# A recurrence stage woven by hand on TensorE, with keys normalised by features

## The chip, the core and the metric

The kernel runs on one core of a Trainium2 chip. A core has TensorE (PE), VectorE (DVE), ScalarE (ACT), GpSimd (POOL) and SyncE (SP), which here issues the loads; each engine works through its own instructions in order and waits on semaphores for the others. The metric is the time of one execution in device microseconds, in the median of several runs.

## What is computed

Two blocks follow each other. The first, which the change touches, projects 528 rows of 1024 features and runs a convolution branch and an RWKV-7 recurrence beside each other; the second (two layers of attention and a mixture of experts) is left as it was. All is fp32. The part that matters:

```python
h = layer_norm(concat([meta, x]))                  # 528 x 1024
p = h @ w_in                                       # conv, r k v, decay/rate/gate, gates
y_conv = conformer_conv(p[..., :c_end])            # GLU, 31 taps, layer norm over features, silu
# rwkv7_time_mix, 16 heads of 64:
p = p + (token_shift(p) - p) * mu
kk = k * k_k
kk = kk / maximum(sqrt(sum(kk * kk, axis=-1)), 1e-12)      # per head
k  = k * (1 + (a - 1) * k_a)
S_t = S_{t-1} diag(decay_t) + (S_{t-1} a_t) b_t^T + v_t k_t^T ;  y_t = S_t r_t   # a = -kk, b = kk * a
o = layer_norm(o) + sum(r * k * r_k) * v ;  o = o * g
y = sigmoid(gate1) * y_conv + sigmoid(gate2) * (o @ w_out)
```

## The kernel before

The recurrence is done in chunks of 64 rows (nine per head, the first half empty), for eight pairs of heads. Every pair j goes through these functions, and a loop of ten steps in first_block calls them for different pairs: at step s, rw_b, rw_solve and rw_bonus for pair s-1, then rw_merge, rw_c and rw_out for pair s-2, then rw_a for pair s.

- rw_a (L358) makes three dense products (k, r, v) of 128 features with all 528 rows, each through token_shift (L289) and dense_ft (L279), then the decays (lw, cum), the keys' squares sq and their sums over a head (ss, L404: five products with two columns), the factor rn per row and head (L410, L411) and the two operands BKf (L426) and AR (L427). A dense product in fp32 is 2 halves of 264 columns x 8 k-tiles x 3 matmuls (hi x hi, lo x hi, hi x lo; L154 to L156), 48 in all.
- rw_b (L445) multiplies AR with BKf per chunk (gr, L460), scales and masks every 128x128 result on DVE (G, L463, 18 of them), writes two parts of G to DRAM (dA, L467) and reads them back in another layout (Dt, L474). It transposes v and BKf (vt, bkt, L480 to L490; BK is scaled by rn at L491) and forms px and at.
- rw_solve (L516) inverts the 16x16 triangles: 15 pairs of a product and a sum on DVE (L524, L525), each on the result of the last; its result goes through DRAM (img) too. rw_merge (L540) builds 64x64 inverses out of them (pm).
- rw_c (L584) forms pB, pG, pM, pN and then a chain of seven small products pS (L642), each with an update of S on DVE (L643), then psy. rw_out (L657) normalises (gsm, gvar, yc) and transposes back (yt, L677).
- The same steps carry the convolution: conv_ft (two dense products), conv_taps (L710: 27 operations cacc over 128x516 on DVE for each of eight filters, L724), conv_norm (L740: the mean and then the variance over all features, each by products as, L737), and gate_ft (16 products in the last steps).
- ada (L1200) hands out weight slabs of the second block: one adw buffer of 512 KB, 8 small matmuls (L1163), a copy adm, and after each second slab two transposes (L1172) and sums on DVE. Nine slabs go with a step.

PSUM has two buffers for dense products (mm), two for the recurrence's g tiles, two for c (pS, yt, pb), one for psy's halves each and one for ada. What orders the instructions is the Tile framework's scheduler with costs of its own: for every engine, PE included, it picks what it holds to be ready, so the functions of one step are interleaved by it. SP issues all loads in one order.

Of the kernel before, what the change touches and what calls it, by code (L numbers as in the profile page):

```python
# [43 lines left out]
            {"yh0": 1, "yl0": 1, "S0": 1, "xg0": 1})  # L44
ADA_FRONT, ADA_EACH, ADA_CONV, ADA_MID = 12, 1, 3, 10
# [27 lines left out]
class K:  # L73
# [204 lines left out]

    def dense_ft(self, ws, m0, m, xs, halves, sink, kts=range(KT), tag="mm"):  # L279
# [78 lines left out]
    def rw_a(self, j):  # L358
# [11 lines left out]
        for q, dst in ((1, k[:, PADL:]), (0, r[:, PADL:]), (2, v[:, 64 + PADL:])):  # L370
            ws = self.weights()
            self.token_shift(ws, 0, 128, 8 * q + j, dst)
            self.ada(ADA_EACH)
# [4 lines left out]


# [17 lines left out]
        kk = wt("kk")  # L397
        nc.scalar.activation(kk, k, AF.Copy, scale=self.col("k_k", j))
        sq = wt("sq")
        nc.scalar.activation(sq, kk, AF.Square)  # L400
        ss = self.psm.tile([128, 512], F32, name="ss", tag="g")
# [3 lines left out]
        rn = self.rn[j % 2]  # L405
        s["rn"] = rn
        st = rw.tile([128, 5, 2], F32, name="sst", tag="sst")
        ssv = ss[:, 0:10].rearrange("p (m h) -> p m h", h=2)
        for lo, hi, m in ((0, 64, 5), (64, 128, 4)):
            nc.vector.tensor_scalar(st[lo:hi, 0:m], ssv[lo:hi, 0:m], 1e-24, 2.0, op0=ALU.max, op1=ALU.mult)  # L410
            nc.vector.reciprocal(rn[lo:hi, lo // 64::2, :], st[lo:hi, 0:m])  # L411
# [5 lines left out]
        nc.vector.scalar_tensor_tensor(b, ta, 1.0, kk, op0=ALU.add, op1=ALU.mult)  # L417
# [27 lines left out]
    def rw_b(self, j):  # L445
# [3 lines left out]
        BKf, AR, rn, v = s["BKf"], s["AR"], s["rn"], s["v"]  # L449
# [4 lines left out]
        for c0 in range(0, 9, 4):  # L454
# [20 lines left out]
        s["Dt"] = Dt  # L475
        for g in range(2):
# [28 lines left out]
        for lo, c0 in ((0, 2), (64, 1)):  # L505
            nc.scalar.activation(UV[lo:lo + 64, c0::2], ps[lo:lo + 64], AF.Copy)
# [508 lines left out]
    def first_block(self):  # L1015
# [51 lines left out]
        for step in range(10):  # L1067
            if 1 <= step <= 8:
                self.rw_b(step - 1)
# [1036 lines left out]
```

## Time and profile before

| | us |
|---|---|
| runs (median of 3) | 4317.6 (4300.29 to 4318.19) |
| profiled execution: time, span | 4312.15, 4310.3 |
| granted PE clock, mean over the span | 0.955 |
| PE, DVE, ACT, POOL busy in the span | 3913.5, 1976.4, 1271.9, 489.9 |
| PE and DVE busy, 209.1 to 639.5 us | 362.60, 335.11 of 430.40 |

The stage of the change runs from about 112 to 896 us. "Busy" of PE counts pipelined matmuls whose ends are modelled; the granted clock is the share of 2.4 GHz, so 0.50 is 1.2 GHz. Idle time is put down to the semaphore that came last. The first gr of the eight pairs started at 150.7, 209.1, 298.7, 382.1, 467.7, 549.8, 639.5 and 734.4 us; "a step" below is the time between two of them.

### The profile page before, as it was taken

Reading aid. Unit: us, or ns where it says so; the run is one execution under the profiler, and the core shown is the slowest. Engines: PE = TensorE matmul, PEld = TensorE weight load, DVE = VectorE, ACT = ScalarE, POOL = GpSimd, SP = SyncE. Lnnn points to the kernel's source line nnn. Section 1 sums busy time; section 2 is a strip of 40 time slices with the busy share of each in tenths; the row PEclk is TensorE's granted clock in tenths of the full one; section 3 lists DMA queues with packets and bytes.
Section 4 is the critical chain, followed back from the end, with each engine's and each line's share of the span. In section 5 each row is a group of like instructions: output and inputs, shape, how many; then the busy total and the mean of one; then the engine's idle time right before and its main releaser. Section 6 shows DMA issues by size and latency. Waiting matters only on the chain. (4 is left out here: it accounts for less than half of the span.)

```text
span 4310.3 us, 68272 instructions
## 1 busy us (share of the span) xinstructions
PE 3913.5 (91%) x28323; PEld 2835.7 (66%) x28323; DVE 1976.4 (46%) x4067; ACT 1271.9 (30%) x2361; POOL 489.9 (11%) x472
## 2 busy tenths in 40 slices
PE   6888888888999899999999899999899999879887
PEld 4767777788998678777878544334577777643322
DVE  4777777644554443445436422213433554432222
ACT  3333333433553333333222211111333332221111
POOL 0322222222010010000003100000010000300000
PEclk9989888999999999999999899999999999989999
DMA  7544454555333222121243698788432124589998
GB/s 233 150 133 121 113 138 135 144 169 164 122 94 102 84 70 64 53 63 53 86 156 118 251 361 323 299 332 318 150 78 65 59 77 147 187 322 409 409 409 333
DMA packets 618041, 764.24 MB, mean 177 GB/s; under 512 B 65593, under 2 KB 463919, under 8 KB 617731
## 3 DMA queue, kind: packets, MB, share of 16 engines
q1 hardware_dynamic: 603699, 722.52, 49.7%
q0 software_dynamic: 6720, 24.87, 1.6%
q10 hardware_dynamic: 7312, 12.48, 0.8%
q8 instruction: 223, 3.65, 0.4%
q14 instruction: 87, 0.71, 0.1%
HBM read 700.45 MB, written 59.33 MB: 176 GB/s over the span
## 5 line engine op out<-in xcount | busy, mean ns | idle before, releaser
L120 DVE TENSOR_TENSOR wlo<-raw,whi 128x1024 fp32r<-128x1024 f32 (+2 forms) x283 | 339.5, 1200 | 606.1 <-ACT whi L118 599.0
L154 PE MATMUL mm<-h2T_hi,whi 128*128 128x512 f32 (+1 forms) x1488 | 526.4, 354 | 2.6 <-ACT kT L1353 2.6
L154 PE MATMUL mm<-hT_hi,whi 128*128 128x258 f32 (+1 forms) x1776 | 521.3, 294 | 5.0 <-ACT gt L775 3.7
L156 PE MATMUL mm<-h2T_hi,wlo 128*128 128x512 f32 (+1 forms) x1488 | 524.0, 352 | 0.0
L155 PE MATMUL mm<-h2T_lo,whi 128*128 128x512 f32 (+1 forms) x1488 | 523.3, 352 | 0.0
L156 PE MATMUL mm<-hT_hi,wlo 128*128 128x258 f32 (+1 forms) x1776 | 518.4, 292 | 1.6 <-DVE wlo L120 1.6
L155 PE MATMUL mm<-hT_lo,whi 128*128 128x258 f32 (+1 forms) x1776 | 517.7, 292 | 0.9 <-POOL hT_lo L786 0.9
L118 ACT ACTIVATE whi<-raw 128x1024 fp32r<-128x1024 f32 (+2 forms) x311 | 306.3, 985 | 686.0 <-PE mm L155 578.2
L1732 PE MATMUL h<-we,xin 128*64 128x512 f32 x1960 | 477.6, 602 | 14.7 <-DMA we<-in_w_e_dram 14.7
L154 PEld LDWEIGHTS mm<-hT_hi,whi 128*128 128x128 f32 x1776 | 342.8, 193 | 13.7 <-issue 4.7
L156 PEld LDWEIGHTS mm<-hT_hi,wlo 128*128 128x128 f32 x1776 | 343.3, 193 | 6.5 <-DVE wlo L120 2.0
L155 PEld LDWEIGHTS mm<-hT_lo,whi 128*128 128x128 f32 x1776 | 343.7, 194 | 5.7 <-issue 2.4
L1732 PEld LDWEIGHTS h<-we,xin 128*64 128x64 f32 x1960 | 143.6, 137 | 291.1 <-issue 253.2
L154 PEld LDWEIGHTS mm<-h2T_hi,whi 128*128 128x128 f32 x1488 | 282.3, 190 | 48.3 <-issue 10.1
L1732 PE MATMUL ye<-we,hT 128*64 128x512 f32 (+1 forms) x2048 | 303.5, 494 | 10.1 <-ACT hT L1809 8.1
L155 PEld LDWEIGHTS mm<-h2T_lo,whi 128*128 128x128 f32 x1488 | 282.4, 190 | 38.7 <-issue 7.6
L156 PEld LDWEIGHTS mm<-h2T_hi,wlo 128*128 128x128 f32 x1488 | 282.4, 190 | 38.3 <-issue 6.5
L1732 PEld LDWEIGHTS ye<-we,hT 128*64 128x64 f32 (+1 forms) x2048 | 103.5, 124 | 184.7 <-issue 128.6
L724 DVE SCALAR_TENSOR_TENSOR cacc<-cc,cdw,cacc 128x516 f32<-128x516 f32 x216 | 178.1, 825 | 3.1
L1804 DVE TENSOR_TENSOR s<-h,s 128x512 f32<-128x512 f32 x32 | 22.1, 692 | 341.3 <-PE h L1732 341.3
L1824 ACT ACTIVATE yh<-y 64x512 fp32r<-64x512 f32 (+1 forms) x128 | 66.7, 521 | 350.9 <-DVE y L1817 348.9
L1817 DVE SCALAR_TENSOR_TENSOR y<-ye,gate,gr 128x512 f32<-128x512 f32 (+1 forms) x48 | 31.7, 661 | 219.6 <-PE ye L1732 219.5
(531 smaller groups left out, 6556.1 us busy)
## 6 DMA issues: line engine op xcount, KB each, us to landing
we<-in_w_e_dram SPq DMA_DIRECT2D x363, 1024.0 KB
raw<-in_w_in_dram SPq DMA_DIRECT2D x170, 512.0 KB
adw<-in_w_ada_dram SPq DMA_DIRECT2D x96, 512.0 KB
raw<-in_ffn_up_dram SPq DMA_DIRECT2D x44, 512.0 KB
raw<-in_w_branch_dram SPq DMA_DIRECT2D x48, 256.0 KB
cres<-in_w_e_dram SPq DMA_DIRECT2D x11, 1024.0 KB
we<-in_w_e_dram POOLq DMA_DIRECT2D x10, 1024.0 KB, 21.2
g_d<-g SPq DMA_DIRECT2D x24, 384.0 KB
```

What stands on the lines that cost most here:

```text
L118: nc.scalar.activation(hi, raw, AF.Copy)
L120: eng.tensor_tensor(lo, raw, hi.bitcast(F32), op=ALU.subtract)
L154: mm(ps, wh, xh, start=(i == 0), stop=False)
L155: mm(ps, wh, xl, start=False, stop=False)
L156: mm(ps, wl, xh, start=False, stop=(i == last))
L724: nc.vector.scalar_tensor_tensor(acc, tap(t), col(t), acc, op0=ALU.mult, op1=ALU.add)
L1732: mm(out[p.cap * g:p.cap * g + p.cap, 0:W], lhs(k), rhs(k)[:, W * d:W * d + W], start=k == 0, stop=k == KT - 1, tile_position=(0, p.cap * g))
L1804: nc.vector.tensor_tensor(s1, p.h3[:, 0:W], s1, op=ALU.mult)
L1817: nc.vector.scalar_tensor_tensor(y, ye[:, 0:W], p.gate, p.gr[:, turn], op0=ALU.mult, op1=ALU.mult)
L1824: nc.scalar.activation(p.yh[r, d], y[r], AF.Copy)
```

## The change

PE's order in the stage is now written out. The pieces of rw_b, rw_merge, rw_c and rw_out become generators; weave (new) takes them in turn from a list, and after every piece it draws one or two units of dense work (nine, nine or six matmuls) from a second generator, fillers, which holds the step's dense products. WEAVE gives the units per step. The loop has 11 steps; rw_out runs one step later, its normalisation is moved to the end of rw_c; rw_solve is emitted right behind the Dt loads; conv_norm starts at step 9, in three parts, and the last filter's taps are emitted ahead of step 8. ada's slabs are drawn inside the dense products' sinks.

The keys are normalised by features: the squares are summed by a product with a block matrix bones, so that the sum stands in every feature row, and the reciprocal multiplies kk there. BKf holds it then, and G is only masked (4 chunks in one operation) and BK only copied, on ACT.

```diff
+WEAVE = (30, 30, 30, 30, 30, 30, 30, 42, 36, 48, 0)
...
+    def dense_units(self, ws, m0, m, xs, halves, sink, tag="mm"):
+        for i, (t0, n) in enumerate(halves):
+            ps = self.psm.tile([128, 512], F32, name="mm", tag=tag)
+            for k in range(KT):
...
+                mm(out, wh, xh, start=k == 0, stop=False)
+                mm(out, wh, xl, start=False, stop=False)
+                mm(out, wl, xh, start=False, stop=k == KT - 1)
+                if k in (2, 5):
+                    yield
+            sink(i, ps[0:m, 0:n], t0, n)
+            yield
...
+        rnb = wt("rnb")
+        for t0 in (0, NTT // 2):
+            ss = self.psm.tile([128, 512], F32, name="ss", tag="mm")
+            mm(ss[:, 0:NTT // 2], self.cst["bones"], sq[:, t0:t0 + NTT // 2], start=True, stop=True)
+            nc.vector.tensor_scalar(rnb[:, t0:t0 + NTT // 2], ss[:, 0:NTT // 2], 1e-24, 2.0, op0=ALU.max, op1=ALU.mult)
+        nc.vector.reciprocal(rnb, rnb)
+        nc.vector.tensor_tensor(rnb, rnb, kk, op=ALU.mult)
...
-        for m in range(5):
-            n = 128 if m < 4 else 64
-            mm(ss[0:n, 2 * m:2 * m + 2], sq[:, 128 * m:128 * m + n], self.cst["hsel"], start=True, stop=True)
...
-            nc.vector.tensor_scalar(st[lo:hi, 0:m], ssv[lo:hi, 0:m], 1e-24, 2.0, op0=ALU.max, op1=ALU.mult)
-            nc.vector.reciprocal(rn[lo:hi, lo // 64::2, :], st[lo:hi, 0:m])
...
-        nc.vector.scalar_tensor_tensor(b, ta, 1.0, kk, op0=ALU.add, op1=ALU.mult)
+        nc.vector.scalar_tensor_tensor(b, ta, 1.0, rnb, op0=ALU.add, op1=ALU.mult)
...
-            for i in range(n):
-                for h in range(2):
-                    nc.vector.scalar_tensor_tensor(G[:, c0 + i, h], ps[h][:, i], rn[:, c0 + i, h:h + 1], self.cst["gmask"], op0=ALU.mult, op1=ALU.mult)
+            for h in range(2):
+                nc.vector.tensor_tensor(G[:, c0:c0 + n, h], ps[h][:, 0:n], self.cst["gmask"].unsqueeze(1).to_broadcast([128, n, 128]), op=ALU.mult)
+            yield
...
         s["Dt"] = Dt
+        self.rw_solve(j)
...
-            nc.vector.tensor_tensor(
-                BK[:, c0:c0 + n].rearrange("p c (h f) -> p c h f", h=2), ps[:, 0:n].rearrange("p c (h f) -> p c h f", h=2),
-                rn[:, c0:c0 + n].unsqueeze(3).to_broadcast([128, n, 2, 64]), op=ALU.mult)
+            nc.scalar.activation(BK[:, c0:c0 + n], ps[:, 0:n], AF.Copy)
+            yield
...
+    def fillers(self, step):
+        if step < 8:
+            yield from self.rw_a(step)
+        if step < 10:
+            for f in CONV[step + 1]:
+                yield from self.conv_ft(f)
+            for f in range(GATES[step], GATES[step + 1]):
+                yield from self.gate_ft(f)
+
+    def weave(self, step):
+        early = self.rw_b(step - 1) if 1 <= step <= 8 else iter(())
+        late = self.rw_late(step - 2) if 2 <= step <= 9 else iter(())
+        out = self.rw_out(step - 3) if step >= 3 else iter(())
+        turns = [early, late, early, out, late, early, late, early, late, early, late, early, late, early, early, late, early, late, early]
+        turns += [late] * 9
+        if step == CONV_NORM + 1:
+            norm = self.conv_norm()
+            turns = [norm] + turns[0:8] + [norm] + turns[8:] + [norm]
...
+        for i, g in enumerate(turns):
+            if next(g, done) is done:
+                continue
+            want = units * (i + 1) // len(turns) - units * i // len(turns)
+            for _ in range(want):
+                next(fill, None)
+        for g in [early, late, out, fill]:
+            for _ in g:
+                pass
...
+        with self.tc.manual_schedule(engines={PE}):
+            self.pinned = True
+            for step in range(11):
+                if step == CONV_NORM:
+                    for f in pending:
+                        self.conv_taps(f)
+                    pending = []
+                self.weave(step)
+                for f in pending:
+                    self.conv_taps(f)
+                pending = CONV[step + 1] if step < 10 else []
```

How this moves instructions is seen at two places. The first is VectorE in a middle step, from behind the masks of one pair to the start of its solve. In the kernel before (bons is the bonus of the pair, k a shifted projection, T and Tt the inverses of the pair ahead, Xt the solve):

```order
L1177 TENSOR_TENSOR mod_214<-mod_214,adb_211 128x2
L442 TENSOR_TENSOR bons<-pb,v 128x258 x2
L724 SCALAR_TENSOR_TENSOR cacc<-cc,cdw,cacc 128x516
L301 SCALAR_TENSOR_TENSOR k<-praw,par,ptmp 128x528
L724 SCALAR_TENSOR_TENSOR cacc<-cc,cdw,cacc 128x516 x3
L565 TENSOR_TENSOR T<-pm_5763,T 128x512
L568 TENSOR_TENSOR Tt<-pm_5780,Tt 32x8x32 x2
L724 SCALAR_TENSOR_TENSOR cacc<-cc,cdw,cacc 128x516
L524 TENSOR_TENSOR Xt<-X_1068,Dt 72x1
L724 SCALAR_TENSOR_TENSOR cacc<-cc,cdw,cacc 128x516
L525 TENSOR_REDUCE X_1068<-Xt 72x1
```

Here taps (cacc) stand on both sides of the solve's first operations. In the changed kernel (pm and T again of the pair ahead, mod an ada result):

```order
L498 TENSOR_TENSOR G<-gr,cst_fb 128x128 x2
L122 TENSOR_TENSOR wlo<-raw,whi 128x1024
L412 SCALAR_TENSOR_TENSOR k<-praw,par,ptmp 128x528
L626 COPY T<-pm_4641 32x8x32 x2
L1259 TENSOR_REDUCE mod_213<-ada 128x2
L1259 TENSOR_REDUCE mod_214<-ada 128x2
L1260 TENSOR_TENSOR mod_213<-mod_213,adb_211 128x2
L1260 TENSOR_TENSOR mod_214<-mod_214,adb_211 128x2
L565 TENSOR_TENSOR Xt<-X_1067,Dt 72x1
L566 TENSOR_REDUCE X_1067<-Xt 72x1
L565 TENSOR_TENSOR Xt<-X_1067,Dt 72x2x2
```

The last two masks are followed by other stages' results and then by the solve without a tap between them; the taps have moved behind it.

The second place is PE around a pair's first gr in a middle step. Before:

```order
L155 MATMUL mm<-hT_lo,whi 128x264
L156 MATMUL mm<-hT_hi,wlo 128x264
L1172 MATMUL ada<-cst_both,adm 128x128 x2
L460 MATMUL gr<-AR,BKf 128x128 x8
L1163 MATMUL ada<-adw,cT 32x128 x8
L460 MATMUL gr<-AR,BKf 128x128 x8
L1163 MATMUL ada<-adw,cT 32x128 x8
L1172 MATMUL ada<-cst_both,adm 128x128 x2
L460 MATMUL gr<-AR,BKf 128x128 x2
L480 MATMUL vt<-cst_both,v 128x128 x4
L484 MATMUL vt<-cst_both,v 128x128
```

The three groups of gr stand close together, with ada slabs between and no dense product. In the changed kernel:

```order
L1246 MATMUL ada<-adw,cT 32x128 x8
L1255 MATMUL ada<-cst_both,adm 128x128 x2
L1246 MATMUL ada<-adw,cT 32x128 x8
L496 MATMUL gr<-AR,BKf 128x128 x8
L295 MATMUL mm<-hT_hi,whi 128x264
L296 MATMUL mm<-hT_lo,whi 128x264
L297 MATMUL mm<-hT_hi,wlo 128x264
```

Two ada slabs now stand directly ahead of the first gr with only the transposes between them, and behind it comes a piece of nine dense matmuls (mm, of which the first three rows are shown) before anything else of the pair.

## Rows read from the trace of the kernel before

**Rows 1.** Windows of the stage: columns as in the line on top (us).
```profile
core 0: us, PE busy (x) PEld busy (x) DVE busy (x) ACT busy (x) POOL busy (x), PEclk, DMA share, GB/s
209.10:639.50 430.40, 362.60 (x4656) 311.64 (x4656) 335.11 (x765) 150.02 (x304) 116.56 (x135) 0.89 0.47 126
...
150.70:209.10 58.40, 51.47 (x513) 44.94 (x512) 53.41 (x121) 21.03 (x41) 21.92 (x22) 0.97 0.55 149
...
639.50:734.40 94.90, 81.86 (x1005) 69.83 (x1005) 72.87 (x163) 30.75 (x65) 21.94 (x23) 0.85 0.46 126
734.40:895.60 161.20, 136.36 (x1669) 124.49 (x1669) 100.61 (x208) 66.57 (x126) 33.49 (x26) 0.94 0.52 150
```

**Rows 2.** Windows inside one step, same columns.
```profile
293.00:300.00 7.00, 1.33 (x12) 1.36 (x12) 6.88 (x11) 0.42 (x1) 4.93 (x8) 0.50 0.13 31
...
316.00:324.00 8.00, 8.00 (x83) 6.22 (x84) 4.92 (x11) 2.07 (x6) 0.00 (x0) 0.52 0.36 82
324.00:330.00 6.00, 6.00 (x118) 4.76 (x115) 4.47 (x8) 2.87 (x7) 0.19 (x1) 1.00 0.42 119
```

**Rows 3.** Groups on VectorE, 112 to 875 us; busy, mean ns, idle before and releaser.
```profile
L724 DVE SCALAR_TENSOR_TENSOR cacc<-cc,cdw,cacc 128x516 f32<-128x516 f32 x216 | 178.1, 825 | 3.1
L524 DVE TENSOR_TENSOR Xt<-X,Dt 72x1 f32<-72x1 f32 (+14 forms) x120 | 50.7, 422 | 1.8
L120 DVE TENSOR_TENSOR wlo<-raw,whi 128x1024 fp32r<-128x1024 f32 x34 | 42.8, 1258 | 11.2 <-ACT whi L118 9.1 <-PE mm L156 1.9
L463 DVE SCALAR_TENSOR_TENSOR G<-gr,rn,cst_fb 128x128 f32<-128x128 f32 x144 | 40.3, 341 | 7.8 <-PE gr L460 7.8
...
L643 DVE SCALAR_TENSOR_TENSOR S<-pS,pcs,S 128x64 f32<-128x64 f32 x56 | 15.7, 281 | 15.7 <-PE pS L642 15.3
L491 DVE TENSOR_TENSOR BK<-bkt,rn 128x512 f32<-128x512 f32 (+1 forms) x24 | 13.1, 554 | 12.4 <-PE bkt L490 12.4
...
L415 DVE TENSOR_TENSOR m<-k,m 128x576 f32<-128x576 f32 x8 | 6.1, 757 | 0.2
...
L565 DVE TENSOR_TENSOR T<-pm,T 128x512 f32<-128x512 f32 x8 | 5.5, 689 | 1.3 <-PE pm L560 1.2
...
L411 DVE RECIPROCAL rn<-sst 64x10 f32<-64x10 f32 (+1 forms) x16 | 3.3, 203 | 0.5
```

**Rows 4.** Groups on VectorE over the whole span: another reciprocal.
```profile
L1502 DVE RECIPROCAL sm<-sm 128x2 f32<-128x2 f32 x40 | 6.6, 165 | 45.3 <-ACT P L1500 45.3
```

**Rows 5.** Waits of PE, 112 to 895 us: total, times, longest (us).
```profile
PE yt L677 <- DVE yc L673: 23.1, 8, 5.4
PE ada L1163 <- DMA adw<-in_w_ada_dram: 21.2, 19, 2.1
...
PE gr L460 <- DVE BKf L426: 12.2, 3, 6.0
...
PE gr L460 <- DVE G L463: 9.2, 7, 2.2
```

**Rows 6.** Timeline of PE at four places: start, us, instruction, idle before.
```profile
153.89 0.64 PE L1163 MATMUL ada<-adw,cT 128*32 128x128 f32 x16 [0.98 <-DMA adw<-in_w_ada_dram]
...
159.37 0.64 PE L1163 MATMUL ada<-adw,cT 128*32 128x128 f32 x16 [0.40 <-DMA adw<-in_w_ada_dram]
...
298.67 1.72 PE L460 MATMUL gr<-AR,BKf 64*128 64x128 f32 x12 [6.01 <-DVE BKf L426]
...
776.33 0.70 PE L737 MATMUL as<-csum,cst_fb 128*128 128x258 f32 x2
...
776.99 0.28 PE L155 MATMUL mm<-hT_lo,whi 128*128 128x258 f32 x1
777.11 0.28 PE L156 MATMUL mm<-hT_hi,wlo 128*128 128x258 f32 x1
...
811.61 1.89 PE L737 MATMUL as<-csum,cst_fb 128*128 128x258 f32 x4 [2.97 <-POOL csum L753]
```

**Rows 7.** A step's last masks on VectorE, and its Dt loads in SP's queue.
```profile
313.01 0.35 DVE L463 SCALAR_TENSOR_TENSOR G<-gr,rn,cst_fb 128x128 f32<-128x128 f32 x1 [1.38 <-PE gr L460]
...
L474 SPq DMA_DIRECT2D Dt<-dA x8: 322/347/473, 314.1 to 322.9; - x8
```

More of the change, by code (lines that the diff above doesn't have):

```diff
@@ L377, in wt, with shift, sink @@
             return rw.tile([128, NTT], F32, name=name, tag="w")
+        def shift(q, dst):
+            ws = self.weights()
+            p = rw.tile([128, T1 + 1], F32, name="praw", tag="w")
+            nc.gpsimd.memset(p[:, 0:1], 0.0)
+            def sink(i, ps, t0, n):
+                nc.scalar.activation(p[:, 1 + t0:1 + t0 + n], ps, AF.Copy)
+                if i == 0:
+                    self.ada(ADA_EACH)
+            yield from self.dense_units(ws, 0, 128, self.hT, self.H2, sink)
+            tmp = rw.tile([128, T1], F32, name="ptmp", tag="w")
+            nc.scalar.activation(tmp, p[:, 1:], AF.Copy, scale=self.omu[:, 8 * q + j:8 * q + j + 1])
+            nc.vector.scalar_tensor_tensor(dst, p[:, 0:T1], self.par[:, 8 * q + j:8 * q + j + 1], tmp, op0=ALU.mult, op1=ALU.add)
+        yield from shift(1, k[:, PADL:])
+        kk = wt("kk")
+        nc.scalar.activation(kk, k, AF.Copy, scale=self.col("k_k", j))
+        sq = wt("sq")
+        nc.scalar.activation(sq, kk, AF.Square)
+        yield from shift(0, r[:, PADL:])
+        rnb = wt("rnb")
[6 more added lines that the diff above has]
+        yield
+        yield from shift(2, v[:, 64 + PADL:])
         lw = wt("lw")
@@ L695, in sink_g @@
             nc.scalar.activation(th[:, t0:t0 + n], ps, AF.Tanh, scale=0.5)
-        self.dense_ft(wg, 0, 128, self.hT, self.H2, sink_g)
-        self.ada(ADA_CONV)
+            self.ada(1 + i)
+        yield from self.dense_units(wg, 0, 128, self.hT, self.H2, sink_g)
         wv = self.weights()
@@ L704, in sink_v, with rw_late @@
             nc.vector.scalar_tensor_tensor(c[:, 30 + t0:30 + t0 + n], th[:, t0:t0 + n], 1.0, ps, op0=ALU.add, op1=ALU.mult)
-        self.dense_ft(wv, 0, 128, self.hT, self.H2, sink_v)
-        self.ada(ADA_CONV)
+            self.ada(1 + i)
+        yield from self.dense_units(wv, 0, 128, self.hT, self.H2, sink_v)
         self.conv_in[f] = c
+    def fillers(self, step):
[15 more added lines that the diff above has]
+            turns = [norm] + turns[0:8] + [norm] + turns[8:] + [norm]
+        fill = self.fillers(step)
+        done = object()
+        units = WEAVE[step]
+        for i, g in enumerate(turns):
[7 more added lines that the diff above has]
+                pass
+    def rw_late(self, j):
+        yield from self.rw_merge(j)
+        yield from self.rw_c(j)
     def conv_taps(self, f):
@@ L1053, in first_block @@
         self.crs = self.csum
-        self.rn = [fix.tile([128, 9, 2], F32, name=f"rn{i}") for i in range(2)]
         self.X = [fix.tile([72, 16, 16], F32, name=f"X{i}") for i in range(2)]
@@ L1066, in first_block @@
         pending = CONV[0]
-        for step in range(10):
-            if 1 <= step <= 8:
-                self.rw_b(step - 1)
-            if 1 <= step <= 8:
-                self.rw_solve(step - 1)
-                self.rw_bonus(step - 1)
-            if step >= 2:
-                self.rw_merge(step - 2)
-            if step >= 2:
-                self.rw_c(step - 2)
-            if step >= 2:
-                self.rw_out(step - 2)
-            if step < 8:
-                self.rw_a(step)
-            for f in pending:
-                self.conv_taps(f)
-            pending = CONV[step + 1]
-            for f in pending:
-                self.conv_ft(f)
-            if step == CONV_NORM:
-                self.conv_norm()
-            for f in range(GATES[step], GATES[step + 1]):
-                self.gate_ft(f)
+        with self.tc.manual_schedule(engines={PE}):
[9 more added lines that the diff above has]
+                pending = CONV[step + 1] if step < 10 else []
+            self.pinned = False
         self.ada(96 - ADA_MID - self.ada_n)
```

61 lines of the change are left out of this document (38 added, 23 removed).

## The prediction

> **What bounds the kernel now.** I first read the windows of the recurrence stage [rows 1]: the change touches only this stage, some 112 to 896 us of the span, and the instruction orders before and behind it stay as they are. The reader is to see a stage without one full engine. In the five middle steps (209.1 to 639.5 us, 430.4 us, 86.1 each) PE is busy 362.6 us, but at a granted clock of 0.89; VectorE (DVE) is busy 335.1, which is 67.0 per step with 19 idle; ACT and POOL are far off. Then I read PE's clock inside one step [rows 2]: when the scheduler runs out of dense products (here about 293 to 324 us), PE first sits nearly idle (1.33 of 7 us busy) and works at 0.50, half of 2.4 GHz; the stretch 316 to 324 us is wholly busy and still at 0.52, and from 324 on the clock is 1.00. A clock of 0.89 over 430 us means (1 - 0.89) x 2 x 430 = 95 us at 1.2 GHz, so at full clock the same work would need some 362.6 - 47 = 315 us, 63 per step. DVE's 67 are then the larger sum: PE looks like the bound, DVE is close to being it. Third, the costliest groups on DVE [rows 3] and PE's waits [rows 5]: PE waits mostly for DVE results (yt for yc 23.1 us, gr for BKf 12.2, gr for G 9.2) and 21.2 us for adw slabs, nearly nothing for dense weights. The single timeline rows [rows 6, 7] give the latencies.
>
> **Part 1: the weave.** It removes no matmul and moves nearly all of them: the pieces of rw_b, rw_merge, rw_out and rw_c stand in PE's own fixed order with 9 dense matmuls between two of them. Dense matmuls start 0.12 us apart [rows 6], so a piece of nine is 1.1 us. What it can win is the dense-free half-clock stretch; what it can't change is DVE's 67 us per step. So I count a step on DVE, from one pair's first gr to the next.
>
> *Head.* From the order, before the third mask stand on PE 42 dense matmuls (42 x 0.12 = 5.1 us), 18 gr products (2.6, from 12 in 1.72 us at half clock [rows 6], an upper bound), the pieces pm1 to pm3 and yt (about 3, estimated from their counts) and one ada slab (0.64), then a wide mask (0.69): 12.0 to 12.5 us. The solve needs Dt, which goes to DRAM and back: before, the last mask G began at 313.01 us and the last Dt load was issued at 322.9 [rows 7], about 9.5 us later, in a queue that was also blocked by adw loads. In the new order fewer loads stand there, so I take 7.7 (range 7 to 15, the upper end being what the queue costs if it is blocked as before). Dt lands at 20.2 us. DVE has for these 20.2 us only the masks (3.3), a wlo (1.26) and about seven results of other stages (4.5): 9 us. The remaining 11 it idles, since in its own order the whole solve, 30 small operations, comes next and waits for Dt, and the taps stand behind it.
>
> *Rest.* Behind Dt stands what is left of DVE's work, 67.0 - 9 = 58.0, plus waits that the old order has too: 15.7/8 = 2.0 for the S chain and 11.2/8 = 1.4 for wlo [rows 3]. With the key edits below (+1.1) a step is 20.2 + 58.0 + 3.4 + 1.1 = 82.7 us.
>
> *Sum of the steps.* Five middle steps have three taps fewer (135 against 138; 0.825 each [rows 3]): 5 x 82.7 - 2.5 = 411, against 430.4. The step before them has no older pair on the late side: 20.2 + 53.4 - 9 + 1.1 = 65.7, against 58.4: here the old order interleaved the solve with taps, and the new one loses 7. The step behind them (639.5 to 734.4) takes 51 taps instead of 35, because the last filter's taps were pulled ahead: 20.2 + 72.9 + 16 x 0.825 - 9 + 3.4 + 1.1 = 101.8, against 94.9. Together 578.5 against 58.4 + 430.4 + 94.9 = 583.7: **-5 us**, hardly anything. The taps that wait at the solve's back cost what the clock returns.
>
> **Part 2: the tail** (734.4 to 895.6 us, 161.2 us). Here DVE has only 100.6 us of work and PE 136.4, with 24.8 idle, at 0.94 [rows 1]. The dense matmuls behind the last pair's first gr are the same number in both orders (1056 up to the next stage's first transposes), so the tail stays PE's. At full clock its work loses half of (1 - 0.94) x 2 x 161 = 19 us, that is 9.7. Of the 24.8 idle I keep 14: the normalisation of the convolution took 35 us from its first sum over features to its second (776.33 to 811.61 [rows 6]); in the new order it starts one step later and between the two sums stand about 20 us of PE work; without the taps that ran beside it I estimate some 28 for it, so PE stops for 8, and I leave 6 for yt and the last pair's chain. The time is 161.2 - 9.7 - 24.8 + 14 = 140.7: **-20.5 us**. If the normalisation keeps its 35 us, it is 7 more.
>
> **Part 3: keys normalised by features.** Removed per pair on DVE: 18 masks G (40.3/8 = 5.0 us), 3 BK (13.1/8 = 1.6, now copies on ACT, which is busy 150 of 430 us), 2 reciprocals (0.4) [rows 3]. Added: 4 masks over 128x4x128, priced as the 128x512 operation from PSUM (0.689 [rows 3]), and 2 small ones, 3.3 in all; 2 wide max-and-double operations from PSUM on 288 columns (0.42 each, scaled from the same row); one product of 128x576 (0.76, as the row of m); and a RECIPROCAL of 128x576, which the trace doesn't show. Its bounds: from below a plain operation of that width, 0.76; from rows, 203 ns for 9 columns (64x10 and 64x8) against 165 ns for 128x2 [rows 3, 4], a slope of 5.4 ns a column, 203 + 567 x 5.4 = 3.2 us. I take 3.2, since both rows are reciprocals. Sum: 3.3 + 0.84 + 0.76 + 3.2 - 5.0 - 1.6 - 0.4 = **+1.1 us** of DVE per pair (-1.3 at the lower bound), already in the steps. On PE it adds two fp32 products of 288 columns in place of five of 2 columns, a few tenths of a us, which fit under a PE that waits for DVE.
>
> Each wide mask frees its PSUM buffers later than single masks did, but PE has nine dense matmuls there, so I cost it at nothing; without that cover it is 0.7 us for each of two groups, 11 us in all, and lies inside the range.
>
> A rule is worth weighing on the reciprocal. The Trainium skill, "VectorE: DVE Perf Modes", in the part on the fixed hardware budget, says that the hardware divides iteratively, with a repeat count of 8. The measured slope of 5.4 ns a column agrees with several passes, but no row here is wide enough to settle it; what it would make of the time is the third rival.
>
> **Forecast.** -5 - 20.5 = -25.5, rounded to -26, from the profiled execution's 4312.15 us (span 4310.3): **4286 us**. The median of the runs shown, 4317.6, lies 5.5 above that execution, the lowest, 4300.29, 12 below; I count from the profile. About 0.5% (21.6 us) is what a measurement can tell from no change, so the forecast is just outside it.
>
> **Rivals.**
> *A real gain.* If Dt lands earlier or the scheduler's order of DVE still lets taps run in the head, DVE's 11 idle us shrink to half: a step of 77, seven steps give 7 x 5.7 = 40 more, and the tail another 10 with its idle gone: 4286 - 50, about **4236**. For it speaks that PE at full clock needs only 63 us a step [rows 1, 2]; against it DVE's new order, in which nothing stands between the masks and the solve. The Trainium skill, "TensorE: Matmul & The Clock Gate", in the part on what bites in real kernels, makes an idle TensorE the cause of the low clock and advises to keep it busy; the trace agrees at 293 to 300 us (1.33 of 7 busy, 0.50), though 316 to 324 us was busy and still at 0.52.
> *Slower.* The fixed order puts two ada slabs back to back twice a step (behind S6 and just ahead of the next gr). There is one adw buffer: slabs came 153.89 to 159.37 = 5.5 us apart when PE had to wait [rows 6], so the second of each couple holds PE, and all behind it, for 5.5 - 0.64 = 4.8 us: 9.7 per step. Before, the scheduler could put dense work there (only 21.2 us waited in the whole stage). It decides if PE reaches the next pair's first gr later than DVE has its BKf; with 2 to 3 us of slack a step this is 7 x 8 = 56 on the forecast: **4342**, slower than before.
> *The long reciprocal.* Eight passes of a plain operation are 8 x 0.76 = 6.1 us, 2.9 more than I took, in front of the taps on the busy DVE: 8 x 2.9 = 23, **4309**.
> *Nothing.* The steps stay at 86 as the solve's wait grows by 3.5 us, and the normalisation eats the tail's gain: about **4312**.
>
> **How the numbers follow.** Chances: the forecast (4265 to 4305) 0.37; real gain 0.20; nothing 0.15; long reciprocal 0.08; slower 0.20. The range 4225 to 4345 leaves out about half of each outer rival, 2 in 10, and takes in the bounds of Dt (up to 7 us a step, 50 us) and of the reciprocal. Faster by over 0.5% (below 4290.6): of the forecast 0.28, and the gain 0.20, together 0.48. Within 0.5%: 0.09 + 0.15 + 0.08 = 0.32. Slower: 0.20.
>
> **What would show it.** Right: in the middle steps the clock near 1.00, DVE idle about 11 us directly ahead of the solve's first operation, the first gr of successive pairs 80 to 85 us apart, over 95 before the last pair, and a tail near 141. The key edits are right if the 128x576 reciprocal takes about 3.2 us and the wide masks about 0.69. Slower is shown by PE waits for adw well over 21 us, with the second slab of a couple in front; the gain by DVE idle under 10 us a step. The forecast is wrong if the clock still falls to 0.5 in each step, or if PE, not DVE, is what the next pair's first gr waits behind.

## The result, and the profile after

The changed kernel took 4429.3 us in the median of four runs (4414.93 to 4438.68), the kernel before 4316.5 (4300.29 to 4318.19): 1.0267 times as long, 95% interval 1.0226 to 1.0308. A second set of four runs gave 4409.63 us (4408.63 to 4421.78) against 4307.77, and 1.0242 (1.0219 to 1.0265). It is slower by 102 to 113 us, where 4286 us, 26 us under the profiled execution of before, were forecast, and it lies above the range (4225 to 4345). The rival called "slower" named the place, at 4342 us.

The profiled execution took 4436.86 us (span 4435.0). The windows of the changed kernel answer to [rows 1]; columns as there. The lines are the four steps from the third to the seventh gr, then the first step, the last one and the tail:

```profile
352.00:750.60 398.60, 288.54 (x3679) 249.04 (x3676) 287.70 (x563) 125.72 (x254) 90.66 (x112) 0.83 0.40 106
...
193.40:271.30 77.90, 53.29 (x509) 46.23 (x506) 53.64 (x101) 22.47 (x44) 17.07 (x23) 0.85 0.48 130
750.60:855.60 105.00, 81.58 (x1023) 72.47 (x1019) 83.39 (x148) 33.00 (x67) 23.31 (x22) 0.86 0.45 120
855.60:1027.60 172.00, 136.70 (x1654) 127.23 (x1653) 87.76 (x186) 67.16 (x128) 38.64 (x29) 0.90 0.47 130
```

The four steps to the seventh gr take 99.7 us each (398.6/4), and the five that [rows 1] puts together, from the second to the seventh gr, 95.9 (479.3/5) instead of 86.1. In the four PE and DVE are each busy 72 us of a step: both wait more, and the clock fell to 0.83 instead of rising from 0.89. For the whole stage, gr_0 is the first gr of the first pair, "steps" the seven intervals to the last pair's, "tail" from there to the first hT_hi of the next stage; all in us, from the profiled executions, with the median time of the runs:

| kernel | gr_0 | steps | tail | time |
|---|---|---|---|---|
| before | 150.7 | 583.7 | 161.2 | 4316.5 |
| changed | 193.4 | 662.2 | 172.0 | 4429.3 |
| changed, second set (e12) | 184.9 | 660.2 | 170.4 | 4409.6 |

So 78.5 us of the loss lie in the steps, 10.8 in the tail and 34 to 43 ahead of the first gr, where a low clock has a part (e12). Behind the stage, in code that no edit touches, the profiled executions still differ by up to 23 us (3394.6 us in e11, 3417.2 in e4), so the columns and the time of a row need not agree more closely than that. What PE waits for in the stage (112 to 1040 us), to be read against [rows 5]; waited for, us in total, times, longest:

```profile
PE ada L1246 <- DMA adw<-in_w_ada_dram: 63.9, 24, 8.3
PE ada L1255 <- ACT adm L1250: 32.4, 34, 4.3
PE ada L1246 <- DVE mod L1259: 19.4, 5, 7.1
PE ada L1255 <- DVE cacc L818: 13.7, 2, 7.9
PE ada L1246 <- ACT adm L1250: 12.3, 2, 7.9
...
PE yt L734 <- DVE yc L724: 5.8, 2, 4.7
```

The first five lines are 141.7 us of waiting at the ada slabs and their transposes; before, the 21.2 for adw were nearly all of it. The wait at yt, 23.1 before, is down to 5.8. How these waits sit in a step is seen on PE's timeline between 522 and 560 us (start, us, instruction, idle ahead of it and its releaser):

```profile
522.63 0.65 PE L1246 MATMUL ada<-adw,cT 128*32 128x128 f32 x16 [2.64 <-DMA adw<-in_w_ada_dram]
528.56 1.08 PE L1246 MATMUL ada<-adw,cT 128*32 128x128 f32 x16 [5.28 <-DMA adw<-in_w_ada_dram]
...
551.58 0.69 PE L1255 MATMUL ada<-cst_both,adm 128*128 128x128 f32 x2 [3.74 <-ACT adm L1250]
558.66 1.08 PE L1246 MATMUL ada<-adw,cT 128*32 128x128 f32 x16 [6.39 <-DVE mod L1259]
559.67 2.08 PE L496 MATMUL gr<-AR,BKf 64*128 64x128 f32 x16
```

The step began at 459.85. Up to 520 us PE waits for nothing longer than 2.1 us. Then two slabs stand back to back and the second waits 5.28 us for the one adw buffer. At the step's end the transposes wait for ACT's copy, and the last slab waits 6.39 us for DVE's sum mod, which must empty the one PSUM buffer. The next pair's gr stands right behind it. DVE's timeline shows why the sum came late; it stands among the pair ahead's rsqrt operations, in DVE's order behind the taps, and some of these took long. POOL's operations of the same time are the second list:

```profile
553.97 1.19 DVE L63 TENSOR_TENSOR rs_t<-grs 128x10 f32<-128x10 f32 x1
555.19 1.20 DVE L64 TENSOR_TENSOR rs_t<-rs_t,rs_x 128x10 f32<-128x10 f32 x1
...
556.62 0.17 DVE L63 TENSOR_TENSOR rs_t<-grs 128x10 f32<-128x10 f32 x1
...
557.11 0.16 DVE L1259 TENSOR_REDUCE mod<-ada 128x2 f32<-128x8 f32 x1
557.23 1.25 DVE L63 TENSOR_TENSOR rs_t<-grs 128x10 f32<-128x10 f32 x1
558.41 0.15 DVE L1259 TENSOR_REDUCE mod<-ada 128x2 f32<-128x8 f32 x1
```

```profile
553.86 1.27 POOL L823 TENSOR_TENSOR csum<-csum,cacc 128x516 f32<-128x516 f32 x1
555.08 1.27 POOL L814 TENSOR_TENSOR cpt<-cpt,cpu 128x516 f32<-128x516 f32 x1
557.19 1.27 POOL L814 TENSOR_TENSOR cpt<-cpt,cpu 128x516 f32<-128x516 f32 x1 [0.83 <-ACT cpu L813]
```

The same operation on 128x10 took 0.17 us at 556.62, with POOL idle, and 1.19 and 1.25 us where it started just behind a POOL operation and ended with it. The five long ones from 550.52 us on took 7.0 us where five short ones take 0.85; this is about the 6.39 us that the last slab waited (an estimate, no run takes POOL's work away).

What is slow here is a ring of queues, not work: PE's next pair stands behind a slab, the slab behind a DVE sum, the sum behind the rest of DVE's queue, and this one behind POOL.

### The profile page after: what moved, and what is told of

It is laid out like the page before. It is cut to its first block, busy times and chain, and to the rows that moved or that the text cites. A ratio compares the mean times of both kernels' runs of the same rounds, so it can differ in the third digit from the quotient of the medians.

```text
span 4435.0 us, 68076 instructions
## 1 busy us (share of the span) xinstructions
PE 3937.0 (89%) x28275; PEld 2851.4 (64%) x28275; DVE 1994.4 (45%) x3947; ACT 1285.0 (29%) x2385; POOL 480.1 (11%) x470
## 5 line engine op out<-in xcount | busy, mean ns | idle before, releaser
L295 PE MATMUL mm<-hT_hi,whi 128*128 128x264 f32 (+1 forms) x896 | 294.3, 328 | 14.2 <-DVE rnb L425 8.6
L296 PE MATMUL mm<-hT_lo,whi 128*128 128x264 f32 (+1 forms) x896 | 269.3, 301 | 0.0
L297 PE MATMUL mm<-hT_hi,wlo 128*128 128x264 f32 (+1 forms) x896 | 268.5, 300 | 0.0
L156 PE MATMUL mm<-hT_hi,whi 128*128 128x258 f32 (+2 forms) x880 | 250.8, 287 | 12.0 <-ACT hT_hi L881 11.6
L157 PE MATMUL mm<-hT_lo,whi 128*128 128x258 f32 (+2 forms) x880 | 251.1, 286 | 1.2 <-POOL hT_lo L882 1.2
L158 PE MATMUL mm<-hT_hi,wlo 128*128 128x258 f32 (+2 forms) x880 | 250.1, 285 | 0.6 <-DVE wlo L122 0.6
L295 PEld LDWEIGHTS mm<-hT_hi,whi 128*128 128x128 f32 x896 | 185.0, 206 | 29.4 <-DVE rnb L425 10.7
L296 PEld LDWEIGHTS mm<-hT_lo,whi 128*128 128x128 f32 x896 | 185.5, 207 | 0.4
L297 PEld LDWEIGHTS mm<-hT_hi,wlo 128*128 128x128 f32 x896 | 184.7, 206 | 0.0
## 6 DMA issues: line engine op xcount, KB each, us to landing
we<-in_w_e_dram POOLq DMA_DIRECT2D x10, 1024.0 KB, 20.4
```

Source lines behind the costliest of these rows:

```text
L156: mm(ps, wh, xh, start=(i == 0), stop=False)
L157: mm(ps, wh, xl, start=False, stop=False)
L158: mm(ps, wl, xh, start=False, stop=(i == last))
L295: mm(out, wh, xh, start=k == 0, stop=False)
L296: mm(out, wh, xl, start=False, stop=False)
L297: mm(out, wl, xh, start=False, stop=k == KT - 1)
```

## The experiments

The theories: A, the slabs in PE's fixed order make the loss; B, DVE bounds the steps, as the prediction had it; C, the keys by features; later D and E (is the weave the better order without slabs?), and F and G on DVE's work. The table of gr_0, steps and tail for all of them:

| kernel | gr_0 | steps | tail | time (runs of before in the same job) |
|---|---|---|---|---|
| e1 weave, 20 of 63 slabs left in the steps | 157.0 | 539.8 | | |
| e5 before, 13 of 64 slabs left in the steps | 143.8 | 532.0 | | |
| e2 before, keys by features | 165.1 | 622.6 | 158.4 | 4352.5 (4304.7) |
| e11 the same, sums in g | 158.3 | 584.6 | 175.8 | 4328.2 (4307.8) |
| e3 weave, old keys | 166.7 | 672.6 | 171.2 | 4413.3 (4304.7) |
| e4 weave, slabs spread | 150.6 | 595.4 | 183.2 | 4346.7 (4304.7) |
| e6 e4 with old keys | 171.3 | 605.0 | 203.4 | 4372.9 (4309.4) |
| e7 weave, slabs spread by PE time | 150.1 | 604.6 | 189.4 | 4353.1 (4309.4) |
| e8 weave, late transposes | 172.5 | 664.3 | 165.5 | 4409.4 (4309.4) |
| e13 weave, taps first | 181.3 | 661.8 | 167.0 | 4412.6 (4309.7) |
| e9 before, 24 taps on DVE | 150.9 | 586.0 | 154.2 | 4293.2 (4307.8) |
| e10 e4, 24 taps on DVE | 150.6 | 605.7 | 191.1 | 4359.5 (4307.8) |

### e1: the weave, its slabs moved behind it

```diff
             def sink(i, ps, t0, n):
                 nc.scalar.activation(p[:, 1 + t0:1 + t0 + n], ps, AF.Copy)
-                if i == 0:
-                    self.ada(ADA_EACH)
...
-            self.ada(1 + i)
```

> The changed kernel with no ada slab inside the woven stage: the 70 or so slabs are worked off in a row right behind it, so that the time of the whole tells nothing and the steps are what is read. Theory A (slabs): PE's fixed order holds slabs that wait for the one adw buffer, for ACT's copy and for DVE's sums behind the taps, and they stand in front of the next pair's gr; without them the middle steps, 95 to 108 us in the changed kernel, come down to 80 us or less. Theory B (DVE is the bound: 15 us idle at each step's head while it waits for Dt, then 63 us of work): they stay above 92 us. Theory C (keys by features are what costs): they stay above 95 us.

The slabs weren't all gone from the stage: behind the weave nothing fixes their place in PE's order, and the scheduler brought 20 of them forward into the steps (320 matmuls, 16 to a slab), where the changed kernel has 63:

```profile
L1242 PE MATMUL ada<-adw,cT 128*32 128x128 f32 x320 | 20.4, 298 | 8.3 <-issue 5.4 <-DMA adw<-in_w_ada_dram 2.8
```

The steps add up to 539.8 us, against 662.2. One by one they are 45.8, 88.7, 84.2, 81.1, 76.0, 76.0 and 88.0 us: the middle ones lie around theory A's 80 and below B's 92. So the slabs in the fixed order make the loss of the steps, though this run also let the scheduler put taps ahead of the solve on DVE (see e13). PE waits 43.6 us for the next pair's BKf instead, which is the bound that the prediction had in mind.

### e5: the kernel before, its slabs moved behind the stage

```diff
             self.token_shift(ws, 0, 128, 8 * q + j, dst)
-            self.ada(ADA_EACH)
...
-        self.ada(ADA_CONV)
```

> The kernel before, in the scheduler's order, with no ada slab in the recurrence steps (they are worked off behind the stage, so the whole time tells nothing). It is to be read beside the weave without slabs, whose seven intervals between the pairs' first gr add up to 540 us. Theory D (the weave is the better order once slabs are out of its way): the old order stays at 565 to 585 us, since its waits for adw were only 21 us. Theory E (the slabs cost both orders alike, the weave gives nothing): about 540 us or less.

532.0 us, less than the weave's 539.8: theory E's number, though the slabs don't cost both orders alike. Here 13 slabs were brought forward into the steps. The slabs in the steps of e5, of before and of the changed kernel:

```profile
L1160 PE MATMUL ada<-adw,cT 128*32 128x128 f32 x208 | 14.9, 349 | 2.7 <-DMA adw<-in_w_ada_dram 2.7
```

```profile
L1163 PE MATMUL ada<-adw,cT 128*32 128x128 f32 x1024 | 50.1, 314 | 21.6 <-DMA adw<-in_w_ada_dram 20.1 <-issue 1.2
```

```profile
L1246 PE MATMUL ada<-adw,cT 128*32 128x128 f32 x1013 | 49.5, 320 | 94.9 <-DMA adw<-in_w_ada_dram 54.2 <-DVE mod L1259 19.4 <-ACT adm L1250 12.3
```

Windows over the seven steps, first of e1, then of e5:

```profile
157.00:696.80 539.80, 438.15 (x5371) 393.08 (x5371) 447.91 (x825) 198.77 (x381) 148.09 (x177) 0.89 0.36 95
```

```profile
143.80:675.80 532.00, 449.39 (x5300) 402.00 (x5300) 453.54 (x938) 188.91 (x358) 159.03 (x183) 0.88 0.35 91
```

Both orders leave DVE idle for 78 to 92 us, and both have PE at a clock of 0.88 to 0.89. The 51 slabs taken out of the old order saved 583.7 - 532.0 = 51.7 us, 1.0 each; the 43 taken out of the weave saved 662.2 - 539.8 = 122.4, 2.8 each. At 1.0 us a slab, the seven more in e1 make up 7 of the 7.8 us between the two runs. So without slabs the orders come out equal, as far as one profile of each can tell, and the slabs' places in PE's order cost about all of the 78.5 us, some 11 per step (an estimate). The two runs also differ in their keys; the weave with old keys and few slabs was not run.

### e8: only the transposes moved

```diff
                 if q % 2:
+                    if p:                      # p = self.pinned
+                        yield
                     ps = psum()
...
                         nc.tensor.transpose(pv[:, i], m[:, i], self.ident)
+                    if p:
+                        adt = self.adm.tile([128, 2, 128], F32, name="adt", tag="adt")
+                        nc.scalar.activation(adt, pv, AF.Copy)
+                        pv = adt
```

> The changed kernel with its slabs at their places, only the two transposes of a couple moved behind to the next slab's place and their result copied out of PSUM by ACT. It takes away PE's waits for ACT's copy adm and for DVE's sums (78 us in the changed kernel's stage with the waits put down to taps), and leaves those for adw (64 us). If the waits add up, 4350 to 4375 us; if the slabs standing back to back are what counts and the other waits only stand in for them, above 4400 us.

4409.4 us, the same as the second set of the changed kernel, steps 664.3. PE's waits in the stage:

```profile
PE ada L1246 <- DMA adw<-in_w_ada_dram: 62.3, 19, 8.3
PE ada L1258 <- ACT adm L1250: 35.0, 8, 8.7
PE ada L1246 <- ACT adt L1261: 29.1, 28, 4.8
PE ada L1246 <- ACT adm L1250: 13.4, 2, 8.6
```

DVE's sums no longer hold PE, but other waits of the same size stand at the same places (139.8 us together). Taking one releaser out of a slab that must wait anyway changes the name of the wait. Waits put down to different releasers at one place don't add up as prices.

### e13: the taps first

```diff
-                if step == CONV_NORM:
-                    for f in pending:
-                        self.conv_taps(f)
-                    pending = []
-                self.weave(step)
                 for f in pending:
                     self.conv_taps(f)
+                self.weave(step)
```

> The changed kernel with its slabs where they are, and the taps of a filter emitted ahead of the step's weave instead of behind it. In the changed kernel no tap stands between the masks and the end of the solve on DVE in a middle step, all 28 behind it; without slabs (e1) and with spread slabs (e4) the scheduler put 14 to 21 of them ahead of the solve, so those two runs changed DVE's order as well. Here 11 to 22 stand ahead of the solve and the slabs still stand back to back. If the slabs hold PE by themselves, the middle steps stay at 93 us or more and the time at 4390 to 4430 us; if DVE's order is the cause (taps piled up behind the solve, DVE idle 15 us ahead of it), the steps fall to 80 to 88 us and the time to 4310 to 4360 us.

The steps are 661.8 us, as in the changed kernel (662.2), and the time 4412.6. In the changed kernel no tap stands ahead of the solve in six of the seven steps, here 13 to 25 do. With the slabs where they are, DVE's order with every tap behind the solve, which the prediction made its bound, is not what costs. PE's waits again, of e13:

```profile
PE ada L1242 <- DMA adw<-in_w_ada_dram: 63.2, 21, 7.5
PE ada L1251 <- ACT adm L1246: 31.0, 36, 3.9
...
PE ada L1242 <- DVE mod L1255: 13.4, 4, 3.8
...
PE ada L1242 <- DVE mod L1256: 7.3, 2, 4.0
```

The wait for adw is that of the changed kernel (63.9); the four lines together are 114.9 us, where the five were 141.7, and the steps are no shorter for it. So the taps that the scheduler moved along with the slabs in e1 and e4 gain nothing by themselves. Whether the slabs would gain as much with the taps left behind the solve, no run shows.

### e4 and e7: the slabs spread

e4 takes the slabs out of the sinks, gives weave one piece of a slab's work at every second turn, and has ACT copy the transposes (as in e8, into two buffers by turns where e6, e7 and e8 have one); e7 gives one slab per estimated 6.4 us of PE work instead:

```diff
                 next(fill, None)
+            if i % 2 and self.ada_n < 96 - ADA_MID:        # e4
+                self.ada_n += next(self.ada_it)
...
+            self.slab(1.1 + 0.97 * want)                   # e7, in place of it
...
+        if self.ada_n < 96 - ADA_MID and self.work - self.last > (2.0 if self.half else 6.4):
```

> The changed kernel with the slabs taken out of the dense products' ends and put singly behind every second turn of the weave, the two transposes of a couple a turn later than its copy, and their result copied out of PSUM by ACT, so that DVE's late sums hold no PSUM. Theory A: PE's waits at ada, about 150 us in the stage, fall under 40, the middle steps to some 80 to 85 us, the time to 4290 to 4340 us. Theory B: the steps stay above 92 us and the time above 4400 us.

> The weave with keys by features and with the slabs spread by estimated PE time (one per 6.4 us of PE's work, transposes 2 us behind) instead of by turns, where two could stand 4 us apart. Theory A (what is left of the loss is the slabs' waits for the one adw buffer, 47 us of PE in e4): those waits fall under 25 us and the time comes to 4315 to 4335 us. Theory B (DVE's order sets the steps): 4340 us or more.

e4 comes to 4346.7 us, 83 under the changed kernel's first set and 63 under its second, still 1.0099 times the kernel before (1.0064 to 1.0134); its steps are 595.4, with 55 slabs in them. That is just above what theory A allowed, and the middle steps are 82 to 94, not 80 to 85. PE's wait for adw is 47.5 us in e4 (under 40 for all waits at ada were expected) and 30.8 in e7 (under 25). With 4353.1 us e7 falls on theory B's side of its expectation, though e1's steps speak against B: spreading further gained nothing, while waits for other things grew (pS for S 24.2 us in e7, 11.5 in e4); its single buffer for the transposes may have a part in that.

```profile
PE ada L1257 <- DMA adw<-in_w_ada_dram: 30.8, 9, 7.3
PE pm L594 <- DVE G L496: 26.9, 6, 6.0
PE pS L688 <- DVE S L689: 24.2, 6, 8.2
```

Here PE's fixed order waits for masks and for S, where the scheduler's order had something else to do. The tails of both (183 and 189 us) are longer than the changed kernel's 172 too; 12 and 20 slabs stand in them, against 2. Steps and tail together are 744.9 us before, 834.2 in the changed kernel, 778.6 in e4 and 794.0 in e7.

### e2, e11, e3 and e6: the keys

e2 puts only the keys by features, the wide masks and ACT's copies of BK into the old order; e11 changes the sums' PSUM buffer in e2; e3 is the changed kernel with the old keys; e6 is e4 with the old keys (and one buffer for the copied transposes).

```diff
-            ss = self.psm.tile([128, 512], F32, name="ss", tag="mm")    # e2
+            ss = self.psm.tile([128, 512], F32, name="ss", tag="g")     # e11
```

> The kernel before with the keys normalised by features, the wide masks and BK copied by ACT, in the scheduler's order, without the weave. Theories A and B: DVE's work changes by about 1 us per pair (the reciprocal measured 3.74 us in the changed kernel, the wide masks 0.69), so the time stays within 15 us of the kernel before. Theory C: slower by 40 us or more.

> As e2 (the kernel before with keys by features, 48 us slower), but the sums of squares go to the recurrence's PSUM buffers g, where the old small sums stood, instead of the dense products' mm. If the 48 us come from PE waiting at the sums for the squares (52 us in e2) while dense products queue for the buffer, this falls to 4315 to 4330 us and PE's wait at ss under 20 us; if they come from DVE's work (1 to 2 us per pair) and the longer path to BKf, it stays above 4340.

> The changed kernel with the old normalisation of the keys (small sums, rn in the masks G and in BK), all of the weave kept. Theories A and B: 4415 to 4440 us, as the changed kernel, give or take 15. Theory C: at least 40 us under the changed kernel's 4429.

> The weave with the slabs spread as in e4, and with the old normalisation of the keys. If the keys by features cost nothing in the weave (they take 1 us of DVE per pair), 4335 to 4360 us, as e4's 4347; if they cost as in the old order (48 us), about 4300 us.

In the old order the keys cost 47.8 us (1.0103, interval 1.0074 to 1.0132), against under 15 expected; in this order that is theory C's size. PE's largest wait in e2, and in e11:

```profile
PE ss L404 <- ACT sq L400: 52.1, 8, 11.4
```

```profile
PE gr L456 <- DVE mod L1169: 24.7, 5, 8.9
...
PE ss L404 <- ACT sq L400: 6.1, 4, 3.3
```

With the sums in g the wait at ss falls from 52.1 to 6.1 us and the time to 4328.2, 20.4 above before (1.0063, 1.0038 to 1.0087): some 24 of the 48 us were the sums' place in PSUM and on PE. The steps are then as short as before (584.6 against 583.7, with the new wait of 24.7 us at gr inside); what is left lies ahead of the first gr (7.6 us, with PE at 0.69 between 84 and 112 us, see e12) and in the tail (14.6), and DVE's work (about 1.5 us per pair, below) doesn't explain it. In the weave itself old keys gave 4413.3 against 4429.3 and 4409.6 for the new ones: no difference that can be told. In the weave with spread slabs the new keys are 26 us faster (4346.7 against 4372.9). Of this e6's profile has 20.7 ahead of the first gr, where its clock was 0.54 and e4's 1.00, so the time doesn't settle it. The steps and the tail do speak for the new keys (778.6 against 808.4 us), and one wait in e6 stands out:

```profile
PE pm L601 <- DVE G L501: 76.1, 7, 15.3
```

PE waits there for 18 narrow masks between taps; with wide masks (e4) the same wait is 25.7. So this edit hurt the steps of the old order with the sums in mm (622.6 against 583.7), not with the sums in g, and in the spread weave it seems to help. Neither expectation of e6 held: it was slower.

### e9 and e10: less work on DVE

```diff
-CONV_ACT = 3
+CONV_ACT = 6
```

> The kernel before with three more of the 31 taps of every filter on ACT and POOL (24 instead of 27 on DVE), which takes 8 x 3 x 0.825 = 20 us of work from DVE in the recurrence stage. Theory F (DVE's work bounds the steps in the old order too, though PE is busier): 12 to 20 us faster, 4290 to 4297. Theory G (the chains between the engines bound them): within 5 us of the kernel before.

> The same three taps moved in the weave with spread slabs (e4, 4347 us). Theory F: 12 to 20 us faster than e4, 4327 to 4335. Theory G: 4342 to 4352.

e9 is faster than the kernel before: 4293.2 against 4307.8 us, 0.9972 (0.9959 to 0.9985). It is the one version that beats both kernels, by an edit that isn't part of the change. Theory F has the size. Where the gain lies isn't shown: the profiled execution is the slowest of the twelve (4306.06), and it has no gain in the steps (586.0 against 583.7) and 7 us in the tail (154.2 against 161.2). e10 is 13 us slower than e4, against F, and above G's range too. DVE's taps in e9, to be read against [rows 3]:

```profile
L724 DVE SCALAR_TENSOR_TENSOR cacc<-cc,cdw,cacc 128x516 f32<-128x516 f32 x192 | 163.6, 852 | 2.7
```

24 taps fewer saved 14.5 us of busy time, not 20, since the others took 852 ns instead of 825. Less work on DVE shortened the steps of neither order in these profiles; theory F is not shown.

### e12: the changed kernel again

> The changed kernel once more. In its profile PE ran at 0.50 from 84 to 132 us, in products ahead of the stage that both kernels share and that ran at 1.00 in the kernel before; this moved its first gr by 22 us. If the low clock belongs to the kernel, the profile shows 0.50 there again; if it is chance, the clock there may be 1.00, the first gr come at about 172 us and the span be about 4413 us, while the steps stay at 95 to 105 us.

The steps came out the same to 2 us. PE between 84 and 112 us, in products that both kernels issue in one order, was at half clock again. The windows of before, of the changed kernel, and of e12:

```profile
84.00:112.00 28.00, 26.70 (x158) 14.83 (x158) 9.02 (x27) 10.52 (x27) 0.51 (x4) 1.00 0.76 257
```

```profile
84.00:112.00 28.00, 28.00 (x107) 13.65 (x106) 5.09 (x16) 6.24 (x16) 0.00 (x0) 0.50 0.51 170
```

```profile
84.00:112.00 28.00, 28.00 (x108) 13.53 (x106) 5.15 (x18) 6.05 (x15) 0.00 (x0) 0.50 0.51 168
```

From 112 to 132 us it was 0.92 in e12, so the loss there was smaller. The same window was 1.00 in e3, e4, e5, e7, e9 and e10, 0.50 in e1 and e13, 0.54 to 0.88 in e2, e6, e8 and e11. It goes neither with the weave nor with the slabs in a way that these runs show; why it fell stays open. Its price can be read, since PE's order in the changed kernel, in e12 and in e3 is the same up to the slab that follows. That slab in each of them, e3 last, at full clock:

```profile
138.13 0.64 PE L1246 MATMUL ada<-adw,cT 128*32 128x128 f32 x16
```

```profile
127.76 0.65 PE L1246 MATMUL ada<-adw,cT 128*32 128x128 f32 x16
```

```profile
113.38 0.65 PE L1255 MATMUL ada<-adw,cT 128*32 128x128 f32 x16
```

So the low clock cost the changed kernel 24.7 us in its first profile and 14.4 in its second. Without it the kernel would still be slower by far.

## Why the prediction was wrong

**What bounds the kernel.** The prediction said that PE looks like the bound and DVE is close to being it. Steps with few slabs support that for neither order: of some 535 us in e5 and e1, DVE is idle 78 and 92, PE 83 and 102.

**The failed step: the steps' sum of -5 us.** It counted a step on DVE (82.7 us) and let PE's fixed order cost nothing; the slabs' waits stood apart in a rival with 0.20. Measured were +78.5 us, by e1 and e5 about all of it from the slabs' places. Its own terms against one measured step (459.85 to 559.70 us):

```profile
459.85:483.90 24.05, 23.09 (x320) 20.44 (x320) 8.76 (x19) 8.81 (x18) 2.31 (x4) 0.89 0.36 84
483.90:559.70 75.80, 49.22 (x603) 42.35 (x601) 62.80 (x116) 22.11 (x45) 18.70 (x23) 0.80 0.39 105
```

The head took 24.05 us to the solve's first operation, 20.2 expected, with 8.76 of DVE work (9 expected). Then the rest was 75.8 us, with 62.8 of work and 13 idle, where 58.0 + 1.1 of work and 3.4 of waits were expected. PE is busy only 49.2 of these 75.8. So the head came out near its size, and 13 of the 17 us that the step came out too long lie behind it. The head's cause was only in part the one given: of DVE's 15.3 idle us none is put down to Dt in this step, and the most to PE's gr.

```profile
DVE G L498 <- PE gr L496: 7.4, 3, 4.7
```

e13 then showed that the head's idle time didn't matter: with taps in it, the steps were as long.

**The rival "slower".** Its mechanism was the cause: two slabs back to back, one adw buffer, the next gr behind them. Its price, 9.7 us a step, is close to the 11 that e1 and e5 give, but by luck: PE's wait for adw in the steps rose from 20.1 to 54.2 us, 4.9 per step, and the rest is what the rival didn't have, ACT's copy and DVE's sum, which hold the same slabs (e8). It also took off a slack of 2 to 3 us, and it set the price on top of a forecast gain; there was no gain below it. The chance of 0.20 was the mistake: the order showed the couples, and the row of 5.5 us between slabs had their price.

**The real gain.** No middle step of the changed kernel came to 77 us (80.7 was the shortest). With few slabs two of the weave's did (76.0), but the old order's seven then average 76.0 as well (532.0/7), so that is no gain of the weave.

**PE's clock.** It was to come near 1.00 in the middle steps and came to 0.83. Before, stretches with little to do had 0.50 [rows 2]; in the changed kernel PE is idle 26.6 of the 75.8 us behind the solve's start, at 0.80, and at 0.89 in the busy head. The Trainium skill, "TensorE: Matmul & The Clock Gate", in the part on what bites in real kernels, lays the low clock to an idle TensorE; these two windows agree; e12's window at 84 us, in which PE was busy for all of 28 us at 0.50, does not. The forecast step of 82.7 us, of which PE needs 63 at full clock, left PE idle for 20 too, so the clock of 1.00 didn't follow from it.

**The tail** (-20.5 forecast, +10.8 measured). The gain rested on a clock of 1.00 and on 11 us less idle. The clock was 0.90, under the 0.94 of before, and PE was idle 35.3 of 172.0 us instead of 24.8: that is nearly the whole loss.

**Ahead of the first gr** the prediction counted nothing, and 43 and 34 us were lost. The low clock of the window above took 24.7 and 14.4 of them. The other 18 to 20 us are the slabs at the dense products' ends again: at full clock there, e3 with the slabs in place has its first gr at 166.7, 16 us behind the kernel before, and e4 with the slabs spread has it at 150.6.

**The keys.** The term of +1.1 us of DVE per pair was about right. The rows of the changed kernel, busy, mean ns, and idle before:

```profile
L426 DVE RECIPROCAL rnb<-rnb 128x576 f32<-128x576 f32 x8 | 29.9, 3743 | 0.1
...
L498 DVE TENSOR_TENSOR G<-gr,cst_fb 128x512 f32<-128x512 f32 (+1 forms) x48 | 25.4, 554 | 36.5 <-PE gr L496 35.9
...
L425 DVE TENSOR_SCALAR rnb<-ss 128x288 f32<-128x288 f32 x16 | 6.9, 447 | 0.2 <-PE ss L424 0.2
...
L427 DVE TENSOR_TENSOR rnb<-rnb,kk 128x576 f32<-128x576 f32 x8 | 6.0, 748 | 0.1
```

3.2 + 0.86 + 0.75 + 3.74 - 5.0 - 1.6 - 0.4 = 1.5 us. The reciprocal took 3.74 us (3.2 expected; the long one, 6.1, is refuted), five times the product of the same width (748 ns). The Trainium skill, "VectorE: DVE Perf Modes", in the part on the fixed hardware budget, speaks of a repeat count of 8; the width's price here, (3743 - 203)/567 = 6.2 ns a column, doesn't speak against several passes, but the whole operation isn't eight plain ones. Where the edit cost time it was outside DVE's work: 48 us in the old order, and 20 once the sums stood in g, none of them in the steps (e2, e11).

## What to carry to other kernels

When PE's order is written by hand, count the side work that sits in it (loads with one buffer, copies on ACT, sums on DVE) first: every such piece holds everything behind it, and the price is the round trip less the work, whenever the engine gets there early. Before a weave is priced, ask what the old order does without that side work; here the two came out equal, and the hand-written order had nothing to win. And look whether the side work really left: in e1 and e5 the scheduler had put 20 and 13 slabs back. A wait's releaser names who came last; a fix that removes only that one moves the wait to the next, so the test is to take the waiting piece out.

## What the runs showed of the hardware

- A fp32 RECIPROCAL of 128x576 on VectorE takes 3.74 us, where a product of two such tiles takes 0.75.
- TensorE can run the same products in the same order at 1.2 or at 2.4 GHz: 28 us of busy PE at 0.50 in two profiles of one kernel, and at 1.00 in the kernel before. The cause stays open.
- Most small VectorE operations that overlap one of GpSimd's end with it: of the 104 rsqrt operations on 128x10 in the changed kernel 80 overlap none and took at most 0.174 us, and of the other 24, 18 end within 0.06 us of GpSimd's operation, after up to 2.25 us.
- The same shows in the taps. In the changed kernel 174 of 216 overlap no GpSimd operation and took 753 ns on average, none over 758; the other 42 took 1303. So more work on GpSimd can cost VectorE time: with its additions for the taps raised from 16 to 40, the taps' mean rose from 825 to 852 ns (e9, with 47 of 192 overlapped against 32 of 216), and in the weave from 881 to 893 (e10 against e4).
